# The order of the first loads, the queue of the pooled stores, a table of turns, and four weight tiles in another ring: a hybrid encoder block on one core

## The chip, the core and the metric

The kernel runs on one NeuronCore of a Trainium2 chip. Its engines work side by side, each on its own list of instructions in order: TensorE (PE) multiplies matrices and transposes into PSUM, VectorE (DVE), ScalarE (ACT) and GpSimd (POOL) work on SBUF and PSUM, and SyncE (SP) sends DMA transfers. ACT and POOL can send transfers too, from queues of their own. The metric is the time of one execution on the device in microseconds (us); lower is better. Each time given as the kernel's is the median of repeated runs.

## The reference

One layer on x (1 x 1024 tokens x 1024 features), everything in float32. Cut to what matters:

```python
h = rms_norm(x, norm1_g)
q, k, v, u = split(h @ w_in)                      # 512 columns each
a = neighbourhood_attention(rms_norm(q), rms_norm(k), v, rpb)   # 8 heads x 64, window 8 x 16 on a 16 x 64 grid
d = mean of u over windows of 2/4/8/16 tokens, minus u          # 4 groups of 128 channels
p = (d @ w_pool per group) * pool_scale
x = x + concat(a, p) @ w_out
h2 = rms_norm(x, norm2_g)
x = x + (silu(h2 @ w_gate) * (h2 @ w_up)) @ w_down               # inner width 2816
```

## The kernel before

Each float32 operand of a matmul is split into a high part, rounded to the type that TensorE takes at full rate, and a low part that holds the rest. A product is three matmuls: high x high, high x low, low x high (`mm3`). `split` makes the two parts: ScalarE casts the high part, VectorE subtracts (its line 112 appears in every profile row of a low part; names end in h and l). All matmuls are on line 85 and all transposes on line 90, so rows are told apart by their tiles.

The tokens lie in 8 tiles of 128, the features in 8 chunks of 128. The heads are done in 4 pairs. The stages in order:

1. Warm-up and first projection. `fetch_first` (line 135) sends the first x chunk `raw_x_0` in two halves from SP's queue, and the small vector `sm_sb` and the first weights `raw_w1_0_0` (two chunks of 384 columns, in halves) from ACT's queue. 17 matmuls on a zeroed tile (`warm`) run meanwhile. Then q, k and v of pair 0 (`pj`) are summed over the chunks k in eight PSUM banks. For chunk 0 the matmuls go in groups of four tokens' tiles: w1h with xh, w1h with xl, w1l with xh. `cook_w1_` and `cook_x_` make w1h, w1l, xh and xl; for the first half of the first weights VectorE also makes the high part (lines 153, 154).
2. The pooled branch (`u_pool`, about 43 to 100 us): `pu` is the projection u, transposed; `u_win` (line 386) sums windows on VectorE (`pw` on line 400; the name stands for another thing in stage 4), multiplies by w_pool (`py`) and stores the high and low part of the result, `yh` and `yl`, to DRAM (`yd`, 512 KB each, line 437). They are read back much later as operands of the output projection (`mx`). The stores of groups 0 to 2 are sent during this stage, those of group 3 in the next.
3. Pairs and attention blocks. `scores`, softmax, `transposes` (`pt`) and `values` (`po`) of 16 blocks (4 a pair) alternate with the projections of the next pair. `step` (line 657) writes a block's parts; between them `more` draws a number of turns from a generator of dense work, `g_dense`. The tables `FIRST`, `CYC` and `WCYC` say how many turns each time. TensorE's order is as written (`pin`). Before the scores of a pair, `proj_shift` (line 329) copies vnh and vnl within SBUF to the shifted tiles vsh and vsl by eight DMA transfers from SP's queue. The normalisation of `e` by the row sums runs on POOL (line 613). The weights of the pair after the next are loaded (`raw_w1_p_k`) and split in between.
4. The output projection (`pw` <- `wo`, `mx`), whose first turns also come from `g_dense`: entry by entry of `WCYC` from the step on in which the projections have ended.
5. Norm 2, transposes to `b_h`, `b_l` and `bt_h`, `bt_l` (PSUM tiles `ht`, `ht_t`; three banks in turn), the gate and up products by a seven-product scheme with sums of weight blocks made on POOL (`sum_w`), and the down projection likewise.

SBUF is handed out by rings: `sp` with 45 slots of 4 KB a partition for nearly all tiles in the order of the program, and from stage 5 on `rg` with 10 slots, for results of gate and up. A tile waits until the former user of its slot is done. Where nothing is pinned a scheduler chooses an engine's order from the program's; `keep` pins ScalarE's and `keepd` VectorE's order to that of the code while their flag is set.

Of the kernel before, what the change touches and what calls it, by code (L numbers as in the profile page):

```python
# [9 lines left out]
F32 = mybir.dt.float32  # L10
F32R = mybir.dt.float32r
AF = mybir.ActivationFunctionType
ALU = mybir.AluOpType
# [3 lines left out]
P = 128  # L17
# [18 lines left out]
R0 = 22  # L36
FIRST = [3, 3, 4, 4, 4, 4, 4, 4, 4, 4, 4]
CYC3 = CYC
WCYC = [1, 3, 3, 2, 2] + [2] * 6 + [3]
POOL_W = [2, 4, 8, 16]  # L40
DGROUPS = [3, 4, 4]
NPF = NFC // 2
# [7 lines left out]
def hybrid_block(ctx, tc, xT, xt, w1, wu, rpbx, wpool, wout, wgu, wd, g2, sm, out):  # L50
    nc = tc.nc
# [3 lines left out]
    yd = [dp.tile([2, P, T], F32, name=f"yd_{g}") for g in range(4)]  # L55
# [7 lines left out]
    def slot(dt, name, shape=None):  # L63
        return sp.tile(shape or [P, 1024], dt, tag="t4", name=name)
# [7 lines left out]
    sm_sb = cp.tile([P, 14], F32, name="sm_sb")  # L72
    g1_sb, psc_sb, gqk = sm_sb[:, 0:8], sm_sb[:, 8:12], sm_sb[:, 12:14]
# [32 lines left out]
    def keepd(i):  # L106
        if pin_dve:
            tc.keep_in_program_order(i)
# [26 lines left out]
    def fetch_first():  # L135
        w = slot(F32, "raw_w1_0_0", [P, 2, 384])
        x = slot(F32, "raw_x_0")
        raws["w1", 0, 0], raws["x", 0] = w, x
        nc.scalar.dma_start(out=sm_sb, in_=sm)
        for i in range(2):  # L140
            nc.sync.dma_start(out=x[:, 512 * i : 512 * i + 512], in_=xT[0][:, 512 * i : 512 * i + 512])
            nc.scalar.dma_start(out=w[:, i], in_=w1[0, :, i, :])

    def cook_w1_(p, kk):
        hs = slot(F32R, f"w1h_{p}_{kk}", [P, 2, 384])
        ls = slot(F32R, f"w1l_{p}_{kk}", [P, 2, 384])
        for i in range(2):
            wp_h[p, 2 * kk + i] = hs[:, i, :]
            wp_l[p, 2 * kk + i] = ls[:, i, :]
        if p == kk == 0:  # L150
            raw = raws.pop(("w1", 0, 0))
            yield
            nc.vector.tensor_copy(hs[:, 0], raw[:, 0])
            nc.vector.tensor_tensor(out=ls[:, 0], in0=raw[:, 0], in1=hs[:, 0].bitcast(F32), op=ALU.subtract)  # L154
            yield
            split(hs[:, 1], ls[:, 1], raw[:, 1])
        else:
            cook(("w1", p, kk), hs, ls)
# [5 lines left out]
    def cook_x_(k):  # L164
        raw = raws.pop(("x", k))
        h = slot(F32R, f"xh_{k}")
        l = slot(F32R, f"xl_{k}")
        n = 512 if k == 0 else T
        for c in range(0, T, n):
            cs = slice(c, c + n)  # L170
            keep(nc.scalar.activation(h[:, cs], raw[:, cs], AF.Copy, scale=g1_sb[:, k : k + 1]))
            nc.vector.scalar_tensor_tensor(
                out=l[:, cs],
                in0=raw[:, cs],
                scalar=g1_sb[:, k : k + 1],
                in1=h[:, cs].bitcast(F32),
                op0=ALU.mult,
                op1=ALU.subtract,
            )
            yield  # L180
        xh.append(h)
        xl.append(l)
# [160 lines left out]
    def u_pool(up, hook):  # L343
# [42 lines left out]
        def u_win(g):  # L386
# [47 lines left out]
            ys = [slot(F32R, f"y{nm}_{g}") for nm in "hl"]  # L434
            split(*ys, y)
            for nm in range(2):
                nc.sync.dma_start(out=yd[g][nm], in_=ys[nm].bitcast(F32))

        for g in range(4):
            if g < 2:  # L440
# [34 lines left out]
        fetch(("xt", t), xt[t], None)  # L475
    fetch_wu(0)
    fetch(("wp",), wpool, [P, 4, P])
    pin_act = True
    for i in range(4):
        if i:  # L480
            cook_w1(0, i)
# [8 lines left out]
    for t in range(NT):  # L490
        raw = raws.pop(("xt", t))
        keep(nc.scalar.activation(raw, raw, AF.Square, accum_out=ssx[:, t : t + 1]))
    pin_act = False
    fetch_wu(1)
    proj_alloc(0)
    pj = [bank(pl, f"pj_0_{t}") for t, pl in enumerate((mmp, mmp, mmp, stp, stp, pop, stp, stp))]
# [511 lines left out]
        sums[i]["s1"], sums[i]["s2"] = s1, s2  # L1008

    def cook_w(i, o):  # L1010
        w = slot(F32R, f"w_{i}_{o}", [P, 2, 512])
        wop[i, o] = w
        if o == "s4":
            x = sums[i]["12"]
            nc.gpsimd.tensor_tensor(out=x, in0=x, in1=sums[i]["s2"], op=ALU.subtract)
        split(w[:, 0], w[:, 1], sums[i][o])
# [390 lines left out]
```

## Time and profile before

| | |
|---|---|
| median of 3 runs | 1016.77 us (1016.56 to 1016.93) |
| the profiled execution | 1018.24 us |
| its span (first to last instruction) | 1016.5 us |
| busy in the span: PE | 999.4 us (98%), 4905 matmuls and transposes |
| DVE | 664.7 us (65%), 1087 instructions |
| ACT | 415.4 us (41%), 817 |
| POOL | 382.7 us (38%), 419 |
| moved by DMA | 136.41 MB, mean 134 GB/s |

Times in rows are microseconds from the start of the span. A row of a timeline gives the start, the length, the engine, the line, what is written <- what is read, and how often in a row; in brackets how long the engine was idle before it and what ended the idle time. SPq, ACTq and POOLq are the queues in which an engine's DMA transfers are issued; the length is that of the issue, not of the transfer. Rows of matmuls overlap a little, since their ends are modelled; the distance of their starts is the better measure.

### The profile page before, as it was taken

The numbers are of one execution on the slowest core, as the hardware profiler recorded it, in microseconds if no ns is written. First come the engines' busy times: TensorE is split into PE (matmuls) and PEld (weight loads), VectorE is DVE, ScalarE is ACT, GpSimd is POOL, SyncE is SP. The second block draws the span as 40 slices with busy tenths as digits, with TensorE's granted clock in tenths as the row PEclk, the third lists the DMA queues.
The fourth block names the chain that finished last, engine by engine and source line by source line (L and its number), as shares of the span: only waits on it lengthen the run. The fifth ranks groups of instructions, "written<-read, shape, count | busy, mean of one in ns | idle before, by whom it ended". The sixth has DMA issues, their size and how long they took to land.

```text
span 1016.5 us, 13484 instructions
## 1 busy us (share of the span) xinstructions
PE 999.4 (98%) x4905; PEld 852.2 (84%) x4905; DVE 664.7 (65%) x1087; ACT 415.4 (41%) x817; POOL 382.7 (38%) x419
## 2 busy tenths in 40 slices
PE   8999989999999998999999999999999999999998
PEld 8988979999788887888888888888888888888887
DVE  5587687656762769766555555555561599988872
ACT  6533476556652436423233233233241354433410
POOL 0000253234330247268657657657643400000170
PEclk9999999999999999999999999999999999999999
DMA  9413633246921322222223223223217984373302
GB/s 357 161 38 119 206 88 112 64 145 212 296 83 42 145 83 94 89 108 104 103 94 114 104 93 114 107 91 114 108 54 229 358 271 160 98 240 119 124 33 93
DMA packets 55298, 136.41 MB, mean 134 GB/s; under 512 B 5888, under 2 KB 14848, under 8 KB 55232
## 3 DMA queue, kind: packets, MB, share of 16 engines
q1 hardware_dynamic: 48016, 110.78, 32.2%
q0 software_dynamic: 5632, 20.19, 5.3%
q10 hardware_dynamic: 1584, 4.60, 1.1%
q8 instruction: 38, 0.62, 0.3%
q14 instruction: 28, 0.23, 0.1%
HBM read 98.57 MB, written 32.77 MB: 129 GB/s over the span
## 4 chain that ended last, share of the span: by engine, by line
PE 90%; DVE 4%; ACT 3%; DMA 2%; issue 1%; SPq 1%; ACTq 0%; DVEq 0%
PE x L85 12%; PE w L85 12%; PE z L85 12%; PE pj L85 9%; PE pw L85 8%; PE pc L85 6%; PE y L85 6%; PE pa L85 6%; PE pd L85 6%; PE pu L85 3%; PE pb L85 3%; PE po L85 3%; DMA raw_w<-in_w 2%; PE s L85 1%; PE pt L90 1%
## 5 line engine op out<-in xcount | busy, mean ns | idle before, releaser
L85 PE MATMUL x<-b_h,w 128*128 128x512 f32 x352 | 115.7, 391 | 0.0
L85 PE MATMUL pj<-w1h,xh 128*128 128x384 f32 x256 | 87.7, 347 | 5.0 <-DVE vnl L293 4.3
L85 PE MATMUL pw<-wo,mx 128*128 128x512 f32 x384 | 91.6, 393 | 0.5 <-DVE kl L112 0.4
L85 PE MATMUL pj<-w1l,xh 128*128 128x384 f32 x256 | 85.0, 336 | 3.2 <-DVE w1l L154 2.2
L613 POOL TENSOR_SCALAR e<-e,r 64x128 f32<-64x128 f32 (+2 forms) x96 | 53.5, 572 | 88.6 <-DVE r L608 50.6
L85 PE MATMUL pj<-w1h,xl 128*128 128x384 f32 x256 | 84.5, 339 | 0.0
L85 PEld LDWEIGHTS pw<-wo,mx 128*128 128x128 f32 x384 | 70.9, 188 | 15.4 <-DVE kl L112 0.8
L1333 POOL TENSOR_TENSOR x2r<-x2r,u 128x512 f32<-128x512 f32 x12 | 23.8, 2020 | 149.8 <-DVE u L1291 149.8
L85 PEld LDWEIGHTS x<-b_h,w 128*128 128x128 f32 x352 | 66.0, 188 | 13.5
L1052 POOL TENSOR_TENSOR ur<-ur,gr 128x512 f32<-128x512 f32 x33 | 52.5, 1592 | 43.4 <-issue 22.0
L85 PE MATMUL x<-b_l,w 128*128 128x512 f32 x176 | 68.8, 391 | 0.0
L112 DVE TENSOR_TENSOR w_s<-sa,w_s 128x512 fp32r<-128x512 f32 x44 | 48.5, 1103 | 25.5 <-ACT w_s L111 25.4
L111 ACT CAST a_h<-raw_a 128x1024 fp32r<-128x1024 f32 (+1 forms) x42 | 41.0, 978 | 50.3 <-PE pc L85 13.8
L85 PE MATMUL w<-b_h,w_s 128*128 128x512 f32 x176 | 57.8, 390 | 0.0
L85 PE MATMUL z<-bt_h,w 128*128 128x512 f32 x176 | 57.8, 389 | 0.0
L85 PE MATMUL z<-bt_h,w_s 128*128 128x512 f32 x176 | 57.8, 389 | 0.0
L85 PE MATMUL y<-bt_h,w_s 128*128 128x512 f32 x176 | 57.8, 389 | 0.0
L85 PE MATMUL w<-bt_h,w_s 128*128 128x512 f32 x176 | 57.8, 389 | 0.0
L85 PEld LDWEIGHTS pj<-w1h,xh 128*128 128x128 f32 x256 | 48.5, 190 | 6.7 <-DVE vnl L293 5.2
L1005 POOL TENSOR_TENSOR sa<-raw_g,raw_g 128x512 f32<-128x512 f32 x11 | 14.6, 1331 | 103.5 <-DMA raw_g<-in_wgu 63.9
L112 DVE TENSOR_TENSOR a_l<-raw_a,a_h 128x1024 fp32r<-128x1024 f32 (+1 forms) x42 | 49.9, 1191 | 3.4 <-ACT a_h L111 3.0
L85 PEld LDWEIGHTS pj<-w1l,xh 128*128 128x128 f32 x256 | 48.0, 188 | 4.1 <-DVE w1l L154 2.7
(256 smaller groups left out, 2684.6 us busy)
## 6 DMA issues: line engine op xcount, KB each, us to landing
raw_a<-gsd SPq DMA_DIRECT2D x77, 256.0 KB, 4.0
raw_g<-in_wgu SPq DMA_DIRECT2D x22, 512.0 KB, 3.6
raw_u<-in_wgu SPq DMA_DIRECT2D x22, 512.0 KB, 3.8
gsd<-gr POOLq DMA_DIRECT2D x22, 512.0 KB, 4.0
raw_d<-in_wd SPq DMA_DIRECT2D x20, 512.0 KB, 4.6
nb<-in_rpbx SPq DMA_DIRECT2D x24, 384.0 KB, 4.1
raw_w<-in_w SPq DMA_DIRECT2D x15, 384.0 KB, 4.6
gsd<-ur POOLq DMA_DIRECT2D x11, 512.0 KB, 3.3
```

The source lines that it names most:

```text
L85: i = nc.tensor.matmul(*a, **k)
L90: i = nc.tensor.transpose(*a)
L111: keep(nc.scalar.copy(h, src))
L112: keepd(nc.vector.tensor_tensor(out=l, in0=src, in1=h.bitcast(F32), op=ALU.subtract))
L613: nc.gpsimd.tensor_scalar(out=out, in0=in0, scalar1=s1, scalar2=1.0, op0=ALU.mult, op1=ALU.mult)
L1005: tt(out=s1, in0=r0[:, 1], in1=r1[:, 1], op=ALU.add)
L1052: eng.tensor_tensor(out=res[i][c][:, l], in0=src, in1=g, op=ALU.mult)
L1333: nc.gpsimd.tensor_tensor(out=q, in0=q, in1=U2[c], op=ALU.add)
```

## The change

The first loads all go from SP's queue, in the turn x half, w half, x half, w half, and only the small vector from ACT's. VectorE's order of the first operands is pinned: the cast of the first weights' first half, then the low part of x's first half, then the low part of the weights. The pooled parts are stored from POOL's queue. `WCYC` gives other numbers of turns. The operand tiles w_0_11, w_0_12, w_1_11 and w_1_12 are taken from the ring `rg` instead of the common slots.

```diff
--- before.py
+++ after.py
@@ -36,7 +36,7 @@
 R0 = 22
 FIRST = [3, 3, 4, 4, 4, 4, 4, 4, 4, 4, 4]
 CYC3 = CYC
-WCYC = [1, 3, 3, 2, 2] + [2] * 6 + [3]
+WCYC = [1, 4, 4, 1, 1] + [2] * 6 + [3]
 POOL_W = [2, 4, 8, 16]
 DGROUPS = [3, 4, 4]
 NPF = NFC // 2
@@ -136,10 +136,11 @@
         w = slot(F32, "raw_w1_0_0", [P, 2, 384])
         x = slot(F32, "raw_x_0")
         raws["w1", 0, 0], raws["x", 0] = w, x
-        nc.scalar.dma_start(out=sm_sb, in_=sm)
         for i in range(2):
             nc.sync.dma_start(out=x[:, 512 * i : 512 * i + 512], in_=xT[0][:, 512 * i : 512 * i + 512])
-            nc.scalar.dma_start(out=w[:, i], in_=w1[0, :, i, :])
+            nc.sync.dma_start(out=w[:, i], in_=w1[0, :, i, :])
+            if i == 0:
+                nc.scalar.dma_start(out=sm_sb, in_=sm)
 
     def cook_w1_(p, kk):
         hs = slot(F32R, f"w1h_{p}_{kk}", [P, 2, 384])
@@ -149,9 +150,11 @@
             wp_l[p, 2 * kk + i] = ls[:, i, :]
         if p == kk == 0:
             raw = raws.pop(("w1", 0, 0))
+            keepd(nc.vector.tensor_copy(hs[:, 0], raw[:, 0]))
             yield
-            nc.vector.tensor_copy(hs[:, 0], raw[:, 0])
-            nc.vector.tensor_tensor(out=ls[:, 0], in0=raw[:, 0], in1=hs[:, 0].bitcast(F32), op=ALU.subtract)
+            keepd(
+                nc.vector.tensor_tensor(out=ls[:, 0], in0=raw[:, 0], in1=hs[:, 0].bitcast(F32), op=ALU.subtract)
+            )
             yield
             split(hs[:, 1], ls[:, 1], raw[:, 1])
         else:
@@ -169,13 +172,15 @@
         for c in range(0, T, n):
             cs = slice(c, c + n)
             keep(nc.scalar.activation(h[:, cs], raw[:, cs], AF.Copy, scale=g1_sb[:, k : k + 1]))
-            nc.vector.scalar_tensor_tensor(
-                out=l[:, cs],
-                in0=raw[:, cs],
-                scalar=g1_sb[:, k : k + 1],
-                in1=h[:, cs].bitcast(F32),
-                op0=ALU.mult,
-                op1=ALU.subtract,
+            keepd(
+                nc.vector.scalar_tensor_tensor(
+                    out=l[:, cs],
+                    in0=raw[:, cs],
+                    scalar=g1_sb[:, k : k + 1],
+                    in1=h[:, cs].bitcast(F32),
+                    op0=ALU.mult,
+                    op1=ALU.subtract,
+                )
             )
             yield
         xh.append(h)
@@ -434,7 +439,7 @@
             ys = [slot(F32R, f"y{nm}_{g}") for nm in "hl"]
             split(*ys, y)
             for nm in range(2):
-                nc.sync.dma_start(out=yd[g][nm], in_=ys[nm].bitcast(F32))
+                nc.gpsimd.dma_start(out=yd[g][nm], in_=ys[nm].bitcast(F32))
 
         for g in range(4):
             if g < 2:
@@ -475,7 +480,7 @@
         fetch(("xt", t), xt[t], None)
     fetch_wu(0)
     fetch(("wp",), wpool, [P, 4, P])
-    pin_act = True
+    pin_act = pin_dve = True
     for i in range(4):
         if i:
             cook_w1(0, i)
@@ -490,7 +495,7 @@
     for t in range(NT):
         raw = raws.pop(("xt", t))
         keep(nc.scalar.activation(raw, raw, AF.Square, accum_out=ssx[:, t : t + 1]))
-    pin_act = False
+    pin_act = pin_dve = False
     fetch_wu(1)
     proj_alloc(0)
     pj = [bank(pl, f"pj_0_{t}") for t, pl in enumerate((mmp, mmp, mmp, stp, stp, pop, stp, stp))]
@@ -1008,7 +1013,10 @@
         sums[i]["s1"], sums[i]["s2"] = s1, s2
 
     def cook_w(i, o):
-        w = slot(F32R, f"w_{i}_{o}", [P, 2, 512])
+        if i < 2 and o in ("11", "12"):
+            w = rg.tile([P, 2, 512], F32R, tag="w", name=f"w_{i}_{o}")
+        else:
+            w = slot(F32R, f"w_{i}_{o}", [P, 2, 512])
         wop[i, o] = w
         if o == "s4":
             x = sums[i]["12"]
```

What this moves is seen in the lists of instructions.

VectorE from the program's start, before (the numbers behind tile names tell copies apart; xl_0 is made in two halves, w1l_0_0 and w1h_0_0 too):

```order
L465 MEMSET warm_100 128x256
L172 SCALAR_TENSOR_TENSOR xl_0_163<-raw_x_0_94,sm_sb_80,xh_0_162 128x512
L153 CAST w1h_0_0_160<-raw_w1_0_0_93 128x384
L172 SCALAR_TENSOR_TENSOR xl_0_163<-raw_x_0_94,sm_sb_80,xh_0_162 128x512
L112 TENSOR_TENSOR w1l_0_0_161<-raw_w1_0_0_93,w1h_0_0_160 128x384
L154 TENSOR_TENSOR w1l_0_0_161<-raw_w1_0_0_93,w1h_0_0_160 128x384
```

and of the change:

```order
L470 MEMSET warm_100 128x256
L153 CAST w1h_0_0_160<-raw_w1_0_0_93 128x384
L176 SCALAR_TENSOR_TENSOR xl_0_164<-raw_x_0_94,sm_sb_80,xh_0_163 128x512
L156 TENSOR_TENSOR w1l_0_0_161<-raw_w1_0_0_93,w1h_0_0_160 128x384
L176 SCALAR_TENSOR_TENSOR xl_0_164<-raw_x_0_94,sm_sb_80,xh_0_163 128x512
L112 TENSOR_TENSOR w1l_0_0_161<-raw_w1_0_0_93,w1h_0_0_160 128x384
```

The low part of the first half (line 154, now 156) stood behind that of the second half (line 112) and now stands two places ahead of it.

SP where the stores of group 3 stood, at the copies to vsh and vsl of pair 0, before:

```order
L564 DMA nb_0_3_0_1495<-in_rpbx 128x768
L437 DMA yd_3_64<-yh_3_1135 128x1024
L334 DMA vsh_0_1158<-vnh_0_227 96x4x128
L335 DMA vsh_0_1158<-vnh_0_227 32x4x128
L437 DMA yd_3_64<-yl_3_1136 128x1024
L336 DMA vsh_0_1158<-vnh_0_227 32x4x128
L337 DMA vsh_0_1158<-vnh_0_227 96x4x128
L334 DMA vsl_0_1159<-vnl_0_228 96x4x128
L335 DMA vsl_0_1159<-vnl_0_228 32x4x128
L336 DMA vsl_0_1159<-vnl_0_228 32x4x128
L337 DMA vsl_0_1159<-vnl_0_228 96x4x128
L119 DMA raw_w1_2_0_1436<-in_w1 128x768
```

and POOL's list where they stand in the change:

```order
L570 TENSOR_SCALAR nb_0_1_1_1215<-nb_0_1_1_1215 128x768
L442 DMA yd_3_64<-yh_3_1135 128x1024
L67 MEMSET mixf_0_1156 128x1
L442 DMA yd_3_64<-yl_3_1136 128x1024
L618 TENSOR_SCALAR e_0_0_0_0_1186<-e_0_0_0_0_1186,r_0_0_0_1185 128x384
L618 TENSOR_SCALAR e_0_0_0_1_1190<-e_0_0_0_1_1190,r_0_0_0_1185 128x384
```

Between SP's copies no store is left; on POOL the last one stands directly ahead of the normalisation of block 0's e. The other six stores moved from SP to POOL in the same way, further ahead.

TensorE in the step in which the last pair's q and k of tokens 6 and 7 are transposed (qkt_3_3), from there to the scores of the last pair, in the change (rows of the pt transposes left out):

```order
L85 MATMUL pw_1_0_0_3196<-wo_3_0_0_3043,mx_6_0_0_2729 128x512
L85 MATMUL pw_1_0_0_3196<-wo_3_0_1_3044,mx_6_0_0_2729 128x512
L85 MATMUL pw_1_0_0_3196<-wo_3_0_0_3043,mx_6_0_1_2730 128x512
L90 MATMUL qkt_3_3_3219<-ident_82,qn_3_6_3073 128x128
L90 MATMUL qkt_3_3_3219<-ident_82,qn_3_7_3077 128x128
```

where before these pw, and three of pw_0 ahead of them, stood behind the transposes:

```order
L85 MATMUL pw_2_0_0_3200<-wo_2_0_0_2995,mx_4_0_1_2647 128x512
L90 MATMUL qkt_3_3_3213<-ident_82,qn_3_6_3073 128x128
L90 MATMUL qkt_3_3_3213<-ident_82,qn_3_7_3077 128x128
L90 MATMUL qkt_3_3_3213<-ident_82,qn_3_6_3073 128x128
L90 MATMUL qkt_3_3_3213<-ident_82,qn_3_7_3077 128x128
```

Six matmuls now stand ahead of qkt_3_3 that stood between pt and the next scores; six of the twelve remain there.

## Rows read from the trace of the kernel before

**Rows 1.** The page's first line.

```profile
span 1016.5 us, 13484 instructions
```

**Rows 2.** TensorE's waits: what it wrote, the engine and line it waited for, in total us, how often, the longest.

```profile
PE pj L85 <- DVE vnl L293: 4.3, 3, 2.6
PE pj L85 <- DVE w1l L154: 2.2, 1, 2.2
PE ht_t L90 <- DVE bt_l L112: 1.5, 1, 1.5
...
PE pj L85 <- DVE w1l L112: 1.1, 1, 1.1
```

**Rows 3.** The timeline of the first 16 us: TensorE, VectorE and ScalarE at the first operands.

```profile
1.19 3.99 PE L85 MATMUL warm_ps<-warm 128*128 128x256 f32 x17 [1.19 <-DVE warm L465]
...
3.91 0.72 ACT L171 ACTIVATE xh<-raw_x,sm_sb 128x512 fp32r<-128x512 f32 x1 [1.89 <-DMA sm_sb<-in_sm]
...
5.13 0.72 ACT L171 ACTIVATE xh<-raw_x,sm_sb 128x512 fp32r<-128x512 f32 x1 [0.50 <-DMA raw_x<-in_xT]
...
5.33 0.35 DVE L153 CAST w1h<-raw_w 128x384 fp32r<-128x384 f32 x1
...
5.83 1.62 PE L85 MATMUL pj<-w1h,xh 128*128 128x384 f32 x4 [0.66 <-DVE w1h L153]
5.88 0.75 DVE L172 SCALAR_TENSOR_TENSOR xl<-raw_x,sm_sb,xh 128x512 fp32r<-128x512 f32 x1 [0.20 <-ACT xh L171]
...
7.25 1.48 PE L85 MATMUL pj<-w1h,xl 128*128 128x384 f32 x4
...
9.27 0.51 ACT L111 CAST w1h<-raw_w 128x384 fp32r<-128x384 f32 x1 [3.42 <-DMA raw_w<-in_w]
...
10.29 0.55 DVE L154 TENSOR_TENSOR w1l<-raw_w,w1h 128x384 fp32r<-128x384 f32 x1
...
10.90 0.96 PE L85 MATMUL pj<-w1l,xh 128*128 128x384 f32 x4 [2.17 <-DVE w1l L154]
...
12.39 0.85 PE L85 MATMUL pj<-w1h,xl 128*128 128x384 f32 x4
...
12.94 2.48 DVE L172 SCALAR_TENSOR_TENSOR xl<-raw_x,sm_sb,xh 128x1024 fp32r<-128x1024 f32 x2
...
13.08 0.85 PE L85 MATMUL pj<-w1l,xh 128*128 128x384 f32 x4
```

**Rows 4.** The timeline of SP's queue: first at the copies of pair 0, with group 3's stores between them, then at those of pair 1.

```profile
112.24 0.38 SPq L437 DMA_DIRECT2D yd<-yh  x1
112.67 0.76 SPq L334 DMA_DIRECT2D vsh<-vnh  x1
...
114.71 0.68 SPq L437 DMA_DIRECT2D yd<-yl  x1
...
119.77 1.72 SPq L337 DMA_DIRECT2D vsl<-vnl  x1
121.59 0.56 SPq L119 DMA_DIRECT2D raw_w<-in_w  x1
...
148.03 0.63 SPq L334 DMA_DIRECT2D vsh<-vnh  x1
...
152.80 0.61 SPq L337 DMA_DIRECT2D vsl<-vnl  x1
```

**Rows 5.** What the load raw_w1_2_0 released: the timeline of ScalarE, VectorE and TensorE.

```profile
126.25 0.83 ACT L111 CAST w1h<-raw_w 128x768 fp32r<-128x768 f32 x1 [6.09 <-DMA raw_w<-in_w]
...
129.44 0.35 DVE L293 SCALAR_TENSOR_TENSOR vnl<-pj,rstd,vnh 128x128 fp32r<-128x128 f32 x1 [0.28 <-ACT vnh L291]
...
126.61 0.60 PE L90 MATMUL qkt<-ident,qn 128*128 128x128 f32 x4
129.85 0.44 PE L85 MATMUL pj<-w1h,xh 128*128 128x384 f32 x1 [2.64 <-DVE vnl L293]
```

**Rows 6.** POOL's timeline at the end of block 0's e, TensorE's first transposes of it, and a row of the tiles that POOL stores later from its own queue (count; shortest, median and longest issue in ns; first and last start).

```profile
116.35 1.65 POOL L613 TENSOR_SCALAR e<-e,r 128x256 f32<-128x256 f32 x4
...
123.44 1.25 PE L90 MATMUL pt<-ident,e 128*128 128x128 f32 x10
...
L1102 POOL DMA_DIRECT2D gsd<-ur x11: 748/751/770, 440.1 to 803.1; - x11
```

**Rows 7.** The timeline of TensorE around qkt_3_3, and VectorE's kl.

```profile
260.70 0.88 PE L90 MATMUL qkt<-ident,qn 128*128 128x128 f32 x4 [0.94 <-DVE qn L278]
...
262.43 2.98 PE L85 MATMUL pw<-wo,mx 128*128 128x512 f32 x12
...
265.62 0.34 PE L85 MATMUL s<-kl,qh 64*128 64x384 f32 x2
...
264.22 0.42 DVE L112 TENSOR_TENSOR kl<-qkt,kh 128x256 fp32r<-128x256 f32 x1
```

**Rows 8.** The timeline of the u stage: VectorE and ScalarE where they waited for TensorE.

```profile
68.51 0.76 DVE L382 TENSOR_TENSOR u<-pu,rstd_bc 128x256 f32<-128x256 f32 x2 [2.79 <-PE pu L85]
...
84.38 1.57 ACT L431 ACTIVATE y<-py,sm_sb 128x256 f32<-128x256 f32 x4 [6.82 <-PE py L85]
```

**Rows 9.** The timeline of TensorE and VectorE between norm and gate.

```profile
387.78 0.66 PE L90 MATMUL ht_t<-ident,x 128*128 128x128 f32 x4 [0.96 <-DVE b_l L112]
...
387.03 1.29 DVE L112 TENSOR_TENSOR b_l<-ht,b_h 128x512 fp32r<-128x512 f32 x2 [0.21 <-ACT b_h L111]
```

## The prediction

> **What bounds the kernel now.** I read the page first: a span of 1016.5 us [rows 1], of which TensorE is busy 999.4. Only its idle time, and whatever lowers its clock, can be saved; matmuls are neither added nor removed here. The next view is the list of TensorE's waits [rows 2], whose longest entries name the places: operands of the first projection pass that came late (w1l, 2.2), a bank of the pair projections that VectorE emptied late (vnl, 4.3 in three waits, 2.6 the longest), the transposes between norm and gate (bt_l 1.5, and 0.96 for b_l [rows 9]), and one wait for w1l that VectorE had not reached (1.1). Then I read the timeline at each place, back from the waiting matmul to what released it.
>
> **The first loads.** The warm-up matmuls run back to back to 5.18 (1.19 + 3.99). The first real ones start at 5.83, behind the CAST of w1h at 5.33, two groups of four pass, and then TensorE stands for 2.17 until w1l is made [rows 3]. What is late is not needed: VectorE's w1l of the first half (10.29) stands behind the w1l of the second half, which waits for ScalarE's cast at 9.27, which waits 3.42 for the second half of the weights, sent from ScalarE's queue. After the change SP sends x half, w half, x half, w half, and VectorE's order is CAST, xl, first w1l.
>
> When does it start now? The two x halves came 1.22 apart (ScalarE starts on them at 3.91 and 5.13 [rows 3]). A w half has three quarters of the bytes of an x half, so behind the first x half I put it 0.9 later, 4.8. The CAST takes 0.35: 5.15, when the warm-up ends at 5.18. The xl that follows takes about 0.75, w1l 0.55: ready at 6.5, while the first four matmuls last until 6.6 and the next four until 8.0. So w1l no longer stops TensorE. The second w half would come near 7 instead of 9.2; only the ninth group and later ask for it. In the old run the operands of chunk 2 were ready at 14.2 (12.94 plus half of 2.48) and TensorE came to them at 17.9 (10.90 plus 40 matmuls of 0.175), so a start up to 3.7 earlier meets no new wait.
>
> What is gained depends on the rate. Before the stall four matmuls took 1.42 (7.25 - 5.83), 0.355 apiece, which is the lower clock level; after it 0.69 (13.08 - 12.39), 0.1725 apiece, the upper one [rows 3]. So the level rose somewhere between 8.7 and 10.9, in or at the end of the idle time. If it rises at the same time as now, say 9.3, then by 10.90 TensorE has done (9.3 - 5.18)/0.355 = 11.6 plus 1.6/0.1725 = 9.3, together 21 matmuls where it had done 8: 13 x 0.1725 = **2.2 us**. If the w half is no earlier than now (5.33 for the CAST), start at 5.83 costs 0.65/0.355 = 2 matmuls of these and the gain is 1.9; if the level rises only at 10.9 it is 8 matmuls and 1.4. If the uninterrupted work brings the upper level from 5.9 on, it is 2 + 29 = 31 done, 23 x 0.1725 = 4.0, cut to 3.7 by chunk 2. I take 2.2, ends 1.4 and 3.7. On this, the Trainium skill ("TensorE: Matmul & The Clock Gate", Part 1) says that the throttled level is the default and that activity releases it; the two rates agree, and by that rule the unbroken run of matmuls favours the upper end.
>
> The shift must live through the u stage. VectorE there waits for TensorE (2.79 before 68.51), and ScalarE too (6.82 before 84.38) [rows 8]; so their chains start earlier by as much, and the later wait for w1l, 1.1 [rows 2], stays as long as it was. It is the work of rows 8 that would give the gain back if it didn't move.
>
> **The pooled stores.** Eight stores of 512 KB move from SP's queue to POOL's. Those of groups 0 to 2 stand where nothing on TensorE waited on SP. Those of group 3 stand among the eight copies that make vsh and vsl [rows 4], ahead of the load raw_w1_2_0. That load is issued at 121.59; ScalarE, in its fixed order, waits 6.09 for it and starts the cast at 126.25, 4.66 later; behind the cast stand the exps, the copy of qn and vnh; VectorE's vnl follows at 129.44 and releases TensorE at 129.85, idle since 127.21 [rows 5]. So the load's time is the wait's time, one for one, down to 127.21.
>
> How much earlier is it issued? The two issues alone are 0.38 and 0.68: **1.1** at the least. The other issues were stretched: eight copies and one store from 112.67 to 121.49 (8.82), where the same eight of the next pair, with nothing between them, take 5.38 (148.03 to 153.41) [rows 4]. If they go as in that quiet round it is 8.82 - 5.38 + 0.38 = 3.8, of which 2.64 can be used here; the rest could at most shorten what is left, 1.7 in the two other waits for vnl together (4.3 less 2.6 [rows 2]). Some of the stretch must stay, since the same bytes go through the same engines at about the same time, only from another queue. I take the middle, 2.5, and of it **2.4** in TensorE's time; ends 1.1 and 3.8.
>
> On POOL the price is the issue. The nearest rows are the later stores of the gate's results, 0.75 each from the same queue [rows 6]. yd_3's two stores now stand ahead of the normalisation of block 0's e, which is done at 118.00 (116.35 + 1.65), and TensorE asks for it at 123.44: 5.4 us of slack against 1.5, so nothing. If that cover were gone it would cost the 1.5.
>
> **The out-projection's table.** Six pw matmuls move ahead of qkt_3_3. TensorE stands 0.94 before it for qn [rows 7]; six take 6 x 0.248 = 1.49 (the twelve from 262.43 took 2.98), so the transposes start at 261.25 (260.70 - 0.94 + 1.49) for 260.70, and all that hangs on them is 0.55 later down to kl: 264.64 becomes 265.19. Behind the pt transposes stand six pw fewer, so the scores would be asked for 0.94 earlier; their second pair, at 265.62, needs kl and can start at 265.2. Gain **0.4**; ends 0 (if kl is 0.4 later still) and 0.94.
>
> **The ring.** Four operand tiles come from the result ring instead of the common slots, so the tile for the first sums is free sooner. POOL's sums start earlier, and the loads of the next gate weights. No matmul waits for either: the waits of 0.96 and 1.5 are the round trip of three banks, transposes to b_h to b_l (387.03) and back [rows 9], in an order that is not changed. **0**; the low end is 0, the high end the 0.96 of b_l, should VectorE be found free earlier. The pins on VectorE add no instruction.
>
> **Sum.** 2.2 + 2.4 + 0.4 + 0 = 5.0. The profiled execution took 1018.24 (span 1016.5), 1.47 above the median; it becomes 1013.2, and the median 1016.77 becomes **1011.8 us**. All low ends give 2.5 (1014.3), all high ends 3.7 + 3.8 + 0.94 + 0.96 = 9.4 (1007.4).
>
> **The rivals.** All times on the median.
> (a) The upper clock level from the start of real work: head 3.7 instead of 2.2, 1010.3. For: no pause between warm-up and work any more. Against: in the old run four microseconds of warm-up alone had not brought it by 8.7. Chance 0.25.
> (b) The head's gain is lost in the u stage. If VectorE's chain ahead of the wait for w1l (1.1 [rows 2]) is led by loads or by its own work instead of TensorE's results, that wait grows by 2.2. Then 1016.77 - 2.8 = 1014.0. Against: the idle times of rows 8, which end on TensorE. Chance 0.12.
> (c) SP stays as slow, the stretch belonging to the copies themselves: 1.1 instead of 2.4, 1013.1. For: the copies of vsl behind the last store were stretched too (1.72 for the last) [rows 4]. Chance 0.15.
> (d) The change doesn't do what it says: the w half is no earlier from SP's queue than from ScalarE's, and the loads of group 2 land as late as before since the stores' bytes compete from POOL's queue just as well: head 1.4, stores 0, the table 0.4, 1015.0, which is no measurable difference. Chance 0.09.
> (e) Slower: POOL works in order, and a store held there holds e. It costs nothing up to 5.4 us, and the run gets measurably slower only if the two stores of group 3 are held 5.4 + 5.0 + 2.0 = 12.4 us; the longest row of such an issue is 0.77. Chance 0.04. The Trainium skill ("SBUF — State Buffer", SBUF: two separate sides) warns that a DMA issued from POOL can't write its descriptors while a VectorE copy holds the shared port, and gives about 0.6 us alone and 3.1 beside one. By that figure two stores would hold POOL for 6.2, 0.8 beyond the slack, and the sum would be 4.2; no row here shows a store held so.
>
> **How the numbers follow.** The forecast as summed has 0.35; a 0.25, b 0.12, c 0.15, d 0.09, e 0.04. A difference of 0.2%, 2.03 us, is about what can be told from no change: faster is below 1014.7, slower above 1018.8. Forecast, a, c and nearly all of b are faster (0.86), d is the same (0.10 with the rest of b), e slower (0.04). The range leaves out e and half of d, and the highest sums above: 1008.3 to 1014.8.
>
> **What would show it.** Right: matmuls from about 5.2 without a gap through the first pass; the load of raw_w1_2_0 issued 2 to 3 earlier relative to the copies, and the wait near 129.85 below 0.5; qkt_3_3 without a wait; the waits between norm and gate as long as they were. Wrong: a wait for w1l at the end of the u stage that grows; pt of block 0 waiting for POOL; a new wait for a bank behind the moved pw. The forecast fails most easily on when the clock level rises and on how much of SP's stretch goes with the stores.

## The result and the profile after

The changed kernel takes 1011.30 us in the median of 5 runs (1010.37 to 1012.15), the kernel before 1016.77 (1016.21 to 1019.63 in its 5 runs). The ratio is 0.9941 with a 95% interval of 0.9925 to 0.9957: 6.0 us faster by the ratio, 5.5 by the medians, where 5.0 was forecast and 1011.8. The sum came out almost right, but three of its four terms did not: the first loads gave more than was forecast, the stores less, the table of turns more.

The page of the profiled execution (1011.3 us, the median itself), its first line and TensorE's busy time, to be held against [rows 1]:

```profile
span 1009.5 us, 13495 instructions
...
PE 997.8 (99%) x4905; PEld 851.1 (84%) x4905; DVE 660.4 (65%) x1087; ACT 415.8 (41%) x817; POOL 387.9 (38%) x427
```

TensorE's waits after (what it wrote, what it waited for, total us, times, longest):

```profile
PE pj L85 <- DVE vnl L298: 1.7, 2, 1.3
PE ht_t L90 <- DVE bt_l L112: 1.5, 1, 1.5
...
PE pj L85 <- DVE w1l L112: 1.0, 1, 1.0
PE ht_t L90 <- DVE b_l L112: 1.0, 1, 1.0
...
PE pj L85 <- ACT xh L174: 0.4, 1, 0.4
```

Against [rows 2]: the wait of 2.2 for the first w1l is gone, of the three for vnl the longest (2.6) is gone, the 0.94 for qn too; the wait for w1l at the end of the u stage (1.1, now 1.0) and the two between norm and gate (1.5, 1.0) stand as they were.

Since TensorE runs nearly the same list in both, the start of the n-th matmul can be compared directly. In the two profiled executions it stands 3.76 us earlier from the end of chunk 1 to the projections of pair 1, 6.3 earlier behind the load raw_w1_2_0, 6.1 before qkt_3_3, 7.3 to 7.4 behind it, and stays so to the end: 3.8 for the head, 2.5 for the stores, 1.2 for the table; the rest (0.2 lost before qkt_3_3, 0.1 gained between norm and gate) nearly cancels. That is 1.5 to 2 us more than the medians differ, and the experiments show why: the profiled execution of the kernel before waited longer than most at the stores' place.

The head after, TensorE and VectorE, to be held against [rows 3]:

```profile
4.17 0.36 DVE L153 CAST w1h<-raw_w 128x384 fp32r<-128x384 f32 x1 [3.04 <-DMA raw_w<-in_w]
...
4.98 1.01 PE L85 MATMUL pj<-w1h,xh 128*128 128x384 f32 x4
5.26 0.55 DVE L156 TENSOR_TENSOR w1l<-raw_w,w1h 128x384 fp32r<-128x384 f32 x1
...
5.82 0.88 PE L85 MATMUL pj<-w1h,xl 128*128 128x384 f32 x4
...
6.54 0.85 PE L85 MATMUL pj<-w1l,xh 128*128 128x384 f32 x4
...
9.88 0.45 PE L85 MATMUL pj<-w1h,xh 128*128 128x384 f32 x1 [0.40 <-ACT xh L174]
```

The w half came in time for a CAST at 4.17 (forecast 4.8, before 5.33), the first real matmul follows the warm-up without a pause, w1l is ready long before the third group asks for it. The second to the fourth group stand 0.72 and less apart, 0.17 to 0.18 apiece: the upper clock level, and within the first group already (0.84 for its four). So chunk 0 ends early enough that TensorE waits 0.40 for the next x chunk, a wait that is new: SP issues that chunk's load at 2.60, behind the four first loads, where it was 1.64 before.

At the stores' place, SP's queue, ScalarE's cast and TensorE, against [rows 4, 5]:

```profile
108.68 0.76 SPq L339 DMA_DIRECT2D vsh<-vnh  x1
...
114.56 0.62 SPq L342 DMA_DIRECT2D vsl<-vnl  x1
115.28 0.55 SPq L119 DMA_DIRECT2D raw_w<-in_w  x1
...
119.90 0.83 ACT L111 CAST w1h<-raw_w 128x768 fp32r<-128x768 f32 x1 [3.46 <-DMA raw_w<-in_w]
...
123.50 0.44 PE L85 MATMUL pj<-w1h,xh 128*128 128x384 f32 x1
```

From the first copy to the load's issue it is 6.60 us instead of 8.92, and the matmul that waited 2.64 waits no more. On POOL a store's issue took 0.53 to 0.71, and block 0's e was in time.

### The profile page after: what moved, and what is told of

The parts are those of the page before. It is cut to its first block, busy times and chain, and to the rows that moved or that the text cites. A ratio compares the mean times of both kernels' runs of the same rounds, so it can differ in the third digit from the quotient of the medians.

```text
span 1009.5 us, 13495 instructions
## 1 busy us (share of the span) xinstructions
PE 997.8 (99%) x4905; PEld 851.1 (84%) x4905; DVE 660.4 (65%) x1087; ACT 415.8 (41%) x817; POOL 387.9 (38%) x427
## 4 chain that ended last, share of the span: by engine, by line
PE 92%; DVE 3%; ACT 2%; DMA 1%; issue 1%; SPq 0%; DVEq 0%
PE x L85 12%; PE z L85 12%; PE w L85 12%; PE pj L85 10%; PE pw L85 8%; PE pc L85 6%; PE pa L85 6%; PE y L85 6%; PE pd L85 6%; PE pu L85 4%; PE pb L85 3%; PE po L85 3%; PE s L85 2%; PE pt L90 1%; DMA raw_w<-in_w 1%
```

## The edits one by one

Each edit alone, put into the kernel before. The four ran on one chip and share its 35 runs of the kernel before (median 1017.37).

**The first loads and VectorE's order of them.** The edit is the diff's first four pieces: `fetch_first`, `cook_w1_`, `cook_x_` and the flag `pin_dve` around them.

> Only the first loads and VectorE's pinned order of them. If the edits add up as the two traces say (TensorE's matmuls after the first pass stood 3.76 earlier, and the same 3.76 at the end of the u stage): 1013.0, with the upper clock level within half a microsecond of the first real matmul. If the level's rise is a matter of the run and not of the kernel: between 1013.0 and 1014.5, and unequal from run to run. If the u stage gives it back: within 0.5 of before, with a longer wait for w1l at its end.

Measured: ratio 0.9962 (0.9946 to 0.9977), 3.9 us. In its trace chunk 1 starts at 9.86, as in the changed kernel (9.88), and the lead stays 3.81 through the u stage: nothing is given back there, the wait for w1l at its end is 1.05. The first expectation holds.

**The stores.**

```diff
-                nc.sync.dma_start(out=yd[g][nm], in_=ys[nm].bitcast(F32))
+                nc.gpsimd.dma_start(out=yd[g][nm], in_=ys[nm].bitcast(F32))
```

> Only the stores from POOL's queue. If the wait near 129.85 went with the stores: that wait gone, TensorE 2.5 earlier from there on, 1014.3. If the gain needed the earlier start of the first edit: less than 1 us, above 1015.8. If POOL's stores hold e: a wait at block 0's pt transposes, above 1016.8.

Measured: ratio 0.9989 (0.9977 to 1.0002), 1.1 us, which its interval doesn't tell from nothing. In its trace the wait at the load is gone, and TensorE's place against the kernel before moves by 2.6 there and 2.8 by the next pair. The time says 1.1 where 2.5 was expected, the trace 2.8: the two disagree until one sees how the wait itself varies (below).

**The table of turns.**

```diff
-WCYC = [1, 3, 3, 2, 2] + [2] * 6 + [3]
+WCYC = [1, 4, 4, 1, 1] + [2] * 6 + [3]
```

> Only the table of turns. By the two traces (6.13 earlier before qkt_3_3, 7.31 behind the next scores): 1.2 faster, 1015.6. By the sum of the prediction: 0.4 faster, 1016.4.

Measured: ratio 0.9987 (0.9971 to 1.0002), 1.3 us; in its trace TensorE moves from 2.7 to 3.9 earlier at qkt_3_3, 1.2, the same as in the changed kernel. The time by itself is not told from nothing; the step in two traces is.

**The ring.**

```diff
-        w = slot(F32R, f"w_{i}_{o}", [P, 2, 512])
+        if i < 2 and o in ("11", "12"):
+            w = rg.tile([P, 2, 512], F32R, tag="w", name=f"w_{i}_{o}")
+        else:
+            w = slot(F32R, f"w_{i}_{o}", [P, 2, 512])
```

> Only the four tiles in the result ring. By the two traces and the prediction: nothing, 0 to 0.1 faster, 1016.7; POOL's sums and the loads of the next gate weights earlier, TensorE's waits of 0.96 and 1.5 as before. If the earlier loads mattered: those waits shorter.

Measured: ratio 1.0002 (0.9986 to 1.0018). In the changed kernel the sums of raw_u start 21 us earlier and the loads 14, 7 of these being the lead of the whole kernel (POOL's sum at 346.80 for 367.64, SP's load of raw_g at 368.31 for 382.33); with the ring alone they start 17 and 10 earlier, 3.5 being its lead. Against [rows 9] the waits are unchanged, in the ring's own trace (0.96 and 1.49) as in the changed kernel's:

```profile
346.80 1.74 POOL L1010 TENSOR_TENSOR sa<-raw_u,raw_u 128x512 f32<-128x512 f32 x1
...
368.31 3.69 SPq L999 DMA_DIRECT2D raw_g<-in_wgu  x2
...
380.41 0.66 PE L90 MATMUL ht_t<-ident,x 128*128 128x128 f32 x4 [0.96 <-DVE b_l L112]
382.56 0.63 PE L90 MATMUL ht_t<-ident,x 128*128 128x128 f32 x4 [1.49 <-DVE bt_l L112]
```

The four ratios give 3.9 + 1.1 + 1.3 - 0.2 = 6.1 us, the whole change 6.0. So nothing shows that one edit needs another; but each of the four has an interval of some 1.5 us to either side, so an effect of one edit on another of 2 or 3 us would not be seen.

## The head: the wait, and the clock behind it

The first matmuls of the programs with the loads as before differ from execution to execution, though their code there is the same. TensorE in the runs with the stores alone, the table alone and the ring alone, in this order:

```profile
5.80 1.62 PE L85 MATMUL pj<-w1h,xh 128*128 128x384 f32 x4 [0.62 <-ACT xh L171]
7.22 1.48 PE L85 MATMUL pj<-w1h,xl 128*128 128x384 f32 x4
10.59 1.65 PE L85 MATMUL pj<-w1l,xh 128*128 128x384 f32 x4 [1.89 <-DVE w1l L154]
12.04 1.48 PE L85 MATMUL pj<-w1h,xh 128*128 128x384 f32 x4
```

```profile
6.67 0.88 PE L85 MATMUL pj<-w1h,xl 128*128 128x384 f32 x4
9.62 1.65 PE L85 MATMUL pj<-w1l,xh 128*128 128x384 f32 x4 [2.07 <-DVE w1l L154]
11.07 1.48 PE L85 MATMUL pj<-w1h,xh 128*128 128x384 f32 x4
```

```profile
5.94 0.95 PE L85 MATMUL pj<-w1h,xh 128*128 128x384 f32 x4 [0.76 <-DVE w1h L153]
...
8.55 0.98 PE L85 MATMUL pj<-w1l,xh 128*128 128x384 f32 x4 [0.95 <-DVE w1l L154]
```

In the first the groups are still at the lower level, some 0.36 apiece, after the wait (12.04 - 10.59 = 1.45 for four); in the second the upper level had come (0.88 for a group at 6.67) and was lost at the wait; in the third, whose wait was half as long, it held. The windows of the second show the loss (us, busy times, then the granted clock in the third column from the end; 0.50 is the lower of the two levels, 1.2 GHz). That column reads 1.00 until a trace's first recorded change, even where matmuls take 0.355 apiece, so the level before it is read from the distance of the starts:

```profile
10.00:12.00 2.00, 2.00 (x7) 2.00 (x7) 2.00 (x3) 2.00 (x3) 0.20 (x2) 0.50 1.05 425
12.00:14.00 2.00, 2.00 (x10) 2.00 (x10) 2.00 (x2) 1.75 (x3) 0.10 (x1) 0.76 1.01 406
```

So the wait costs its own length and, in this one of the four, the level behind it. The start of the 25th real matmul (chunk 1), read from each trace, shows both:

| loads | executions | 25th real matmul starts at |
|---|---|---|
| as before | before, stores, table, ring | 13.78, 15.12, 14.03, 11.46: mean 13.6 |
| in turn, VectorE's order pinned, 17 warm-up matmuls | after, loads alone, and five more below | 9.88, 9.86, 10.22, 10.62, 9.81, 10.53, 10.10: mean 10.1 |

The head is worth 3.5 us by these means, 3.9 by the time. The moment of the rise stands in each trace's record of the clock. In the first row it is 9.34, 14.20, 6.13 (lost at 9.54, back at 12.96) and 5.62; in the second 5.28, 5.06, 7.31, 5.44, 6.37, 5.54 and 4.59, before the third group of real matmuls in all seven. Whether it is the unbroken work that brings it early was tried by a pause.

**A pause between warm-up and work**, the changed kernel with

```diff
-WARM = 17
+WARM = 12
```

The changed kernel itself ran beside it:

> The changed kernel once more, as the base of the runs beside it. 0.994 of before, 1011 to 1012 where before is 1017. If the early rise of the clock belongs to the kernel, the first four real matmuls at 0.17 to 0.21 apiece as before; if it was this one execution, at 0.355.

Measured: ratio 0.9943 (0.9928 to 0.9958). Its first group ran at the lower level (1.28 for four), the third at the upper. By the expectation's own test, 0.17 to 0.21 apiece for the first four, the early rise did not repeat: they took 0.32. What repeats is a rise before the third group, and its moment varies by two microseconds.

> The changed kernel with 12 warm-up matmuls for 17, so that TensorE pauses about 1 us between warm-up (ends near 4.0) and the first real matmul (4.98). If unbroken work from 1.19 brings the clock up by the first real matmul: the level rises later, the first real matmuls at 0.355, 1 to 2 us slower than the changed kernel. If the level follows the run and not the warm-up: no difference in the medians.

Measured: ratio 0.9956 (0.9939 to 0.9972), 1.2 us slower by the medians (1012.43 for 1011.19), within the intervals. One of its six executions took 2033.36, twice the others, for a reason that stays open; the ratio leaves it out, and the median of the other five is 1012.14. TensorE's head:

```profile
4.66 1.62 PE L85 MATMUL pj<-w1h,xh 128*128 128x384 f32 x4 [0.55 <-ACT xh L174]
6.08 1.48 PE L85 MATMUL pj<-w1h,xl 128*128 128x384 f32 x4
7.36 1.48 PE L85 MATMUL pj<-w1l,xh 128*128 128x384 f32 x4
8.64 1.27 PE L85 MATMUL pj<-w1h,xh 128*128 128x384 f32 x4
9.74 0.88 PE L85 MATMUL pj<-w1h,xl 128*128 128x384 f32 x4
```

The real matmuls start earlier than with 17, so the pause is 0.55 and not the 1 us that was meant, and still TensorE reaches chunk 1 only at 11.16, since the level rose only in the fourth group (9.52). With the wait gone but the level late: 11.16 against 13.6 and 10.1, so about 2.4 of the head is the missing wait and about 1.0 the level. That splits one execution against means, and is no more than that. The run has less warm-up work as well as a pause, so it doesn't tell which of the two counts.

**Loads without the order, and the order without the loads.** The two halves of the edit, each in the kernel before. In the first the loads of `fetch_first` alone are changed:

```diff
-        nc.scalar.dma_start(out=sm_sb, in_=sm)
         for i in range(2):
             nc.sync.dma_start(out=x[:, 512 * i : 512 * i + 512], in_=xT[0][:, 512 * i : 512 * i + 512])
-            nc.scalar.dma_start(out=w[:, i], in_=w1[0, :, i, :])
+            nc.sync.dma_start(out=w[:, i], in_=w1[0, :, i, :])
+            if i == 0:
+                nc.scalar.dma_start(out=sm_sb, in_=sm)
```

> The kernel before with the loads in turn on SP, but VectorE's order left to the scheduler, which writes xl ahead of the first cast and the first w1l behind the second, as in the kernel before. If the place of the loads is enough: the 0.38% that loads and order gave together, 1013. If VectorE's order counts too: w1l ready near 8.2, a wait of about 1.5 us before the third group of matmuls, and some 2 us faster than before, 1015.

Measured: ratio 0.9987 (0.9968 to 1.0007), 1.3 us, not told from nothing. VectorE's rows:

```profile
4.58 0.75 DVE L173 SCALAR_TENSOR_TENSOR xl<-raw_x,sm_sb,xh 128x512 fp32r<-128x512 f32 x1 [3.45 <-ACT xh L172]
5.25 0.35 DVE L154 CAST w1h<-raw_w 128x384 fp32r<-128x384 f32 x1
...
7.61 0.55 DVE L155 TENSOR_TENSOR w1l<-raw_w,w1h 128x384 fp32r<-128x384 f32 x1
```

The CAST stands behind xl, so the first real matmul comes at 5.75 although the weights are there; that is the pause again, and the level rose only in the fourth group, at 10.77, with chunk 1 at 12.32. The wait for w1l was hidden by the low rate: it was ready at 8.16, the third group came at 8.45.

In the second only the pins and the place of the CAST are changed (the pieces in `cook_w1_`, `cook_x_` and the flag).

> The kernel before with VectorE's order of the change, but the first weights still from ScalarE's queue. The first real matmul stays near 5.8, no wait for w1l before the third group; the second half of the weights lands near 9.2, so chunk 1 can't start before about 10.9 (it started at 13.8 and, with both, at 9.9). About 2.5 us faster than before, 1014.5. If the clock level is what counts, the gain is nearer to the full 3.9, since the idle 2 us in which the level was lost are gone.

Measured: ratio 0.9981 (0.9966 to 0.9996). In its trace the first real matmul is at 5.56, behind a pause of 0.38, the level rises all the same at 7.03, and chunk 1 starts at 10.49, earlier than expected: VectorE began the w1l of the weights' second half at 8.48 there, where it was 9.82 in the profiled execution of before. 1.9 us is half of what both give, with an interval that reaches from 0.4 to 3.5. Both halves are below the whole, and the order may be the greater part; the times don't tell more.

Over all traces, then: without a pause ahead of the first real matmul the level rose by 7.31 in seven of seven; with one of 0.38 to 0.76 it rose by 7.03 in three (table, ring, order alone) and at 9.34 or later in four (before, stores, loads in turn only, 12 warm-up). That fits a pause that delays the rise; but the lengths of the pauses don't sort the early from the late, so it is likely and not shown.

## The stores: how long the copies take

The eight copies and what stands between them, from the first copy's start, read from SP's rows in all traces:

| stores of group 3 | eight copies done after | load issued after | wait at the load |
|---|---|---|---|
| on SP: before, loads, table, ring | 8.82, 7.60, 6.69, 7.96 | 8.91, 7.69, 6.79, 8.06 | 2.64, 1.47, 0, 1.55 |
| on SP: loads in turn only, order only | 7.14, 9.21 | 7.24, 9.31 | 0.65, 2.90 |
| on SP, changed kernel otherwise | 7.99 | 8.10 | 0.87 |
| on POOL: stores alone, after, after again, 12 warm-up | 7.14, 6.49, 6.51, 7.30 | 7.25, 6.60, 6.62, 7.41 | 0, 0, 0, 0 |
| on POOL, with the trials at the end of the runs | 7.39, 7.41 | 7.50, 7.52 | 0.18, 0 |

The same code takes 6.69 to 9.21, and the wait goes from nothing to 2.90 with it. The run with the table alone, whose stores are on SP as ever, has the row that settles how to read [rows 4]:

```profile
112.12 0.76 SPq L334 DMA_DIRECT2D vsh<-vnh  x1
...
113.88 0.55 SPq L437 DMA_DIRECT2D yd<-yl  x1
...
118.19 0.62 SPq L337 DMA_DIRECT2D vsl<-vnl  x1
118.91 0.56 SPq L119 DMA_DIRECT2D raw_w<-in_w  x1
```

Over the seven executions with the stores on SP the copies take 7.92 in the mean, one store's issue among them, and the wait is 1.44; over the six on POOL it is 7.04 and 0.03. By these means the edit is worth 1.4, which agrees with 1.1 of the edit alone and with the next run. The profiled execution of before had the second longest of seven, 1.2 above the mean; that can account for most of the 1.47 that it took above the median.

**Group 3 back on SP**, the changed kernel with

```diff
-                nc.gpsimd.dma_start(out=yd[g][nm], in_=ys[nm].bitcast(F32))
+                (nc.sync if g == 3 else nc.gpsimd).dma_start(out=yd[g][nm], in_=ys[nm].bitcast(F32))
```

> The changed kernel with group 3's two stores back on SP, groups 0 to 2 on POOL. If group 3's stores are the whole edit: slower than the changed kernel by what the stores alone gave, 1.1 us (0.1%), with a wait for vnl at the load raw_w1_2_0 of 0 to 2.6 us, unequal from run to run. If groups 0 to 2 carry the gain: the time of the changed kernel.

Measured: ratio 0.9960 (0.9946 to 0.9975), 1.9 us slower than the changed kernel beside it by the medians, a wait of 0.87 in its trace. So group 3's two stores carry the edit; that the six others do anything for the time is not seen.

**No bytes beside the copies.**

```diff
-            for nm in range(2):
-                nc.gpsimd.dma_start(out=yd[g][nm], in_=ys[nm].bitcast(F32))
+            for to in ((0,), (1, 3), (2,), ())[g]:
+                for nm in range(2):
+                    nc.gpsimd.dma_start(out=yd[to][nm], in_=ys[nm].bitcast(F32))
```

> The changed kernel, but group 3's parts are not stored: group 1's are stored into their place, some 20 us earlier, so that no store runs beside the copies of vsh and vsl (the pooled part of the last group is left out of the output). If the copies' issues are stretched by the stores' bytes: the eight take 5.4 us as those of the next pair do, against 6.5 to 7.4 in the executions with the stores on POOL. If the stretch belongs to the copies themselves or to other work at that time: 6.5 to 7.4 still. The order of two casts on ScalarE also changes, so the wait itself tells nothing here; time near the changed kernel's, 1010 to 1011.5.

Measured, first and last copy and the load:

```profile
108.25 0.76 SPq L339 DMA_DIRECT2D vsh<-vnh  x1
...
113.09 0.62 SPq L342 DMA_DIRECT2D vsl<-vnl  x1
113.88 0.48 SPq L119 DMA_DIRECT2D raw_w<-in_w  x1
```

5.46 us for the eight, 0.60 to 0.76 each, as in the quiet round of [rows 4]; that round, pair 1's, takes 0.61 to 0.63 a copy in every trace. So the round of copies is stretched by the stores sent beside it, from whichever queue; moving it to POOL saves its two issues on SP (some 1.1) and leaves most of the stretch. The time, ratio 0.9960 (0.9948 to 0.9971) and 1012.67 where 1010 to 1011.5 was expected, is slower than the changed kernel's: with the other order on ScalarE and VectorE a later wait for vnl grew from 1.28 to 1.93, and behind it the clock fell, here in the windows (granted clock third from the end):

```profile
140.00:145.00 5.00, 4.55 (x22) 3.87 (x23) 4.13 (x19) 2.45 (x9) 0.23 (x3) 0.66 0.09 23
```

Against the changed kernel TensorE lost 0.65 in the wait and some 1.4 in what followed: once more a wait that costs more than its length.

## What was tried on top

Two lines of the u stage exchanged, in the changed kernel:

```diff
-                u_win(g - 1)
                 cook_w1(1, g - 1)
+                u_win(g - 1)
```

> The changed kernel with the split of pair 1's weights written ahead of the window sums of the pooled group (two lines of the u stage exchanged), so that VectorE makes w1l one group earlier. If the wait for w1l at the end of the u stage is VectorE's order: the wait of 1.0 gone, 1 us faster than the changed kernel. If VectorE's work as a whole is late there: the wait moves to py or to the next vnl, no difference.

Measured: ratio 0.9938 (0.9923 to 0.9953) beside 0.9943 for the changed kernel. The wait of 1.0 is gone from its trace, a wait of 0.18 came at the load and 0.14 in the u stage; 0.3 us by the medians (1010.89 for 1011.19) where 1 us was expected, which is not told from nothing.

The same, and four banks in turn for the transposes:

```diff
-    banks2 = (mmp, mmp, pop)
+    banks2 = (mmp, mmp, mmp, pop)
...
-            pt = bank(banks2[nbk % 3], f"ht_{o}_{tt}_{q}")
+            pt = bank(banks2[nbk % 4], f"ht_{o}_{tt}_{q}")
```

> The changed kernel with the two lines of the u stage exchanged and four PSUM banks in turn instead of three for the transposes between norm and gate. If those waits (0.96 and 1.5) are the round trip of a bank: both shorter, about 1.5 us, and the drop of the clock level behind them, 1.2 us in about half of the executions, gone too: 0.2% to 0.3% faster than the changed kernel, ratio 0.991 to before. If VectorE and ScalarE are the limit there: the waits only move, ratio 0.994.

Measured: ratio 0.9948 (0.9928 to 0.9968), 1010.72 in the median. The waits only moved:

```profile
PE ht_t L90 <- DVE t L976: 2.3, 1, 2.3
...
PE ht_t L90 <- DVE bt_l L112: 0.3, 1, 0.3
```

2.3 for the operand t of the transposes, made by VectorE, and 0.3 for bt_l, where 1.0 and 1.5 stood: by this trace VectorE is the limit there, not the bank. Neither version is shown to beat the changed kernel.

## Why the prediction was right in the sum, and where it was not

**First loads: 2.2 forecast, 3.5 to 3.9 measured.** The mechanism held: w half earlier, no wait for w1l, no loss in the u stage, so (b) and (d) fell. One thing was not looked at: "a start up to 3.7 earlier meets no new wait" was read from chunk 2 alone, and chunk 1's xh now makes TensorE wait 0.40, in other traces of the same head up to 1.03. The term was mis-sized at the clock: I let the level rise at 9.3 as in the old trace, and it rose between 4.59 and 7.31. That was rival (a), put at 1 in 4. Its ground against, that four microseconds of warm-up alone had not brought the level, read one execution as a rule; the other traces of the same head have it at 5.62, 6.13 and 14.20. The rule of the Trainium skill ("TensorE: Matmul & The Clock Gate", Part 1), that activity releases the throttled level, pointed to the upper end. The traces agree as far as they go: with no pause the upper level was there by 7.31 in all seven executions, with one in three of seven.

**Stores: 2.4 forecast, 1.1 to 1.9 measured.** The step that failed is "the load's time is the wait's time, one for one, down to 127.21": true of that execution, but its wait was 2.64 where the mean is 1.44. And "some of the stretch must stay, since the same bytes go through the same engines" was right, so far that nearly all of it stays, which is near to rival (c), 1.1. Rival (e) fell: POOL's stores took 0.53 to 0.71 to issue. The Trainium skill ("SBUF — State Buffer", SBUF: two separate sides) warns of a POOL store held by a VectorE copy. This run doesn't test that: in its trace VectorE ran no copy beside any of the eight stores.

**Table: 0.4 forecast, 1.2 in two traces.** Two sizes were off. First, the scores' second pair doesn't need kl of the last tokens. TensorE, then VectorE's kl:

```profile
250.60 4.40 PE L85 MATMUL pw<-wo,mx 128*128 128x512 f32 x18 [0.42 <-DVE kl L112]
254.83 0.67 PE L90 MATMUL qkt<-ident,qn 128*128 128x128 f32 x4
...
257.92 0.46 PE L85 MATMUL s<-kh,qh 64*128 64x384 f32 x2
258.20 0.35 PE L85 MATMUL s<-kl,qh 64*128 64x384 f32 x2
...
258.73 0.48 PE L85 MATMUL s<-kl,qh 64*128 64x384 f32 x2
```

```profile
258.13 0.41 DVE L112 TENSOR_TENSOR kl<-qkt,kh 128x256 fp32r<-128x256 f32 x1
```

The pair at 258.20 starts before kl is done (258.54); only the pair at 258.73 reads these columns (`kv[y][js, H : H + 3, ...]`: tokens 6 and 7 lie in the last of four rows of keys, and the first half, H = 0, takes rows 0 to 2). So the whole 0.94 was to be had. Second, with no wait ahead of them the four transposes pass in 0.50 (254.83 to 255.33) where they took 0.72 (260.70 to 261.42), 0.22 more: 0.94 + 0.22 is the 1.2. A third size was off without consequence: six matmuls more cost 1.35 (4.40 for eighteen against 3.05 for twelve in the old trace), not 1.49, which only moves kl.

**Ring: 0 and 0.** As forecast, though the sums and loads moved by much.

So 2.2 + 2.4 + 0.4 stood for about 3.7 + 1.4 + 1.2. The shortfalls in the first and third (1.5 and 0.8) and the excess in the second (1.0) cancel in part; that the forecast was off by only 0.5 us by the medians, 1.0 by the ratio, is partly luck. The profile's own 1.47 above the median had been seen and carried along, but not asked about: most of it can have lain in the very wait that was being priced.

## What to carry to other kernels

A wait in one profiled execution is one draw: before an edit is priced by it, look whether the same code waits as long in another trace, and if the profiled execution is slower than the median, look for the excess in the longest waits first. An idle stretch early in a kernel can cost more than its length, by what the clock does behind it; here loads that let real work follow the warm-up without a gap gave 3.5 us in the traces' means where the pause and the wait that they removed were 0.6 and 1.8. Moving a transfer to another queue freed the issues behind it, but did not undo the stretch that it brings to the issues beside it.

## What was not expected of the hardware

The kernel before took 1013.13 to 1021.08 in 35 runs on one chip, the changed kernel 1010.10 to 1012.40 in ten: the edits took away scatter as much as time. In the traces the head (25th matmul at 11.46 to 15.12) and the wait at the load (0 to 2.90) are what varied most. What still varies is the clock between norm and gate: after the waits of 0.96 and 1.49 the level fell in the second execution of the changed kernel and not in the first (granted clock third from the end, second execution first):

```profile
382.00:384.00 2.00, 1.52 (x9) 1.48 (x10) 1.57 (x4) 0.59 (x1) 0.92 (x1) 0.69 0.82 250
384.00:386.00 2.00, 2.00 (x11) 2.00 (x10) 1.41 (x3) 1.33 (x3) 2.00 (x3) 0.50 0.02 6
```

```profile
384.00:386.00 2.00, 1.90 (x15) 1.43 (x14) 1.94 (x4) 2.00 (x5) 2.00 (x3) 1.00 0.00 0
```

Between norm and gate TensorE lost 1.2 us there against the first execution, and the same in the runs of the loads alone and of the stores alone; of the thirteen traces with these two waits six have the fall. It fell likewise in the run without the stores' bytes, behind a wait of 1.93, and in that of the order alone, behind one of 2.90, but not behind the 2.64 of the kernel before.

The issue of a copy within SBUF on SP took 0.61 to 0.63 us in pair 1's rounds, 0.60 to 0.76 in pair 0's without the stores, and up to 1.82 in pair 0's with a 512 KB store beside it. Not only a store does this: the first copy of pair 2, issued right behind a load from `in_rpbx` (128x768), took 1.32 in the kernel before, 1.47 in the changed one and 1.67 with the loads in turn only. In a round with stores some copies still take 0.6, and the longest of the kernel before (1.72, at 119.77 in [rows 4]) began 0.3 after the last store had landed; what holds the single issue stays open.
